# New durations and a table of priority shifts for a kernel's list scheduler

## The chip, the cores and the metric

The kernel runs on one core of one Trainium2 chip. The metric is the device time of one execution in microseconds (us). TensorE multiplies matrices into PSUM, VectorE and ScalarE work on tiles of 128 partitions, GpSimd does a few elementwise steps and issues small copies, SyncE (its queue is SP) issues most transfers. Each engine executes its own queue strictly in the order in which the program lists its instructions.

## The reference

Two transformer blocks in sequence on one sequence of 512 tokens with 1024 features, all in fp32. The first block has two layers. Layer one mixes with a chunked mLSTM of four heads, layer two with banded softmax attention of twelve heads; both also attend to 256 memory tokens with four heads of 64, and each ends in a convolutional gated feed-forward of width 2816. The second block has one layer: four differential attention heads (two softmaxes, the second taken away with a weight lambda), eight causal heads with a forget gate, and a gated feed-forward.

```python
for l in range(DEPTH):                       # first block, two layers
    h = rmsnorm(x, norm_mix_g[l])
    if l < N_A_LAYERS: ...                   # mLSTM heads, gated by sigmoid(o)
    else: mix_out = band_attention(q, k_pad, v_pad, b_rel_bias[bl])
    mem_out = memory_attention(q_mem, mem, mem_w_kv[l])
    x = x + jnp.concatenate([mix_out, mem_out], axis=-1) @ w_out
    x = x + conv_ffn(rmsnorm(x, norm_ffn_g[l]), ffn_w_up[l], ffn_conv_w[l], ffn_conv_b[l], ffn_w_down[l])
...
p = softmax(where(chunk_mask, s1, NEG)) - lam * softmax(where(chunk_mask, s2, NEG))   # second block
pf = softmax(where(causal, sf, NEG))
```

## The kernel before, in words

Activations stand with features on the partitions: a tile is 128 features by 512 tokens. A product of fp32 accuracy is made of three fp32r matmuls: each operand is split into a rounded upper half and the rest, and `mm3` (L423, L424, L425 in `mm3`; L443 to L445 in `tm`, for results with tokens on the partitions) multiplies upper by upper, upper by lower and lower by upper. Weights come in by SyncE's queue into two buffers (tag `wr`, L403), are rounded by ScalarE or VectorE (tag `wh`, `round`, L383) and have the rounded half taken away by VectorE or GpSimd (tag `wl`, `sub`, L371); both have four buffers.

`run` lays the program down stage by stage: memory keys and values, norm, first mixer (`layer_a`), output projection, feed-forward (`ffn`), the same with `layer_b`, then norms and `block2_attn`, output projection, feed-forward, last norm. In an attention head the scores (`scores`, L559 and L562) go through `softexp` (reduction L574, exponential L577, reciprocal L578), `scale` (L378), transposes (L589) and `put_pt` (L595 on ScalarE, L596 on VectorE), and `pv64` multiplies by the values (L608, L609, sum of two halves at L611 and L612). A key tile (`build_k`) is copied to the other partitions by two pairs of small transfers from GpSimd's queue (L551, L552).

What stands in each engine's queue is not the program order. The program is traced twice. In the first pass `Order` takes every instruction with its operands, gives each a duration (`duration`) and simulates the engines: an instruction becomes ready when its inputs are done plus a latency, and each engine that falls free takes the ready instruction with the lowest key among up to 60 whose tile buffers can be had (`can`: buffers of one tag are handed out in program order). The key is the position in the program plus what `prio` adds (50 for the first norm, 600 for one set of gates). Where an engine other than TensorE finds nothing, `other` lets it take a step that was made with `either` (round, sub, scale) from VectorE's or ScalarE's backlog. In the second pass the program is traced again with the engines so chosen, and the order of each engine is fixed.

Of the kernel before, what the change touches and what calls it, by code (L numbers as in the profile page):

```python
# [47 lines left out]
class Order:  # L48
# [7 lines left out]
    LAT = {"PE": 200, "DVE": 130, "Activation": 140, "Pool": 80, "SP": 0}  # L56
    SETS = {"Exp": "el", "Tanh": "e", "Silu": "s", "Sqrt": "q", "Ln": "l"}

    def __init__(self, nc, insts, bufs, flex, late):
# [3 lines left out]
        for ins in insts:  # L63
            e = ins.engine.name
            if e not in self.LAT or ins.opcode in ("TilePoolBoundary", "RegisterMove"):
                continue
            self.ops.append(ins)
# [7 lines left out]
        self.cost = [self.duration(k) for k in range(n)]  # L75
# [3 lines left out]
        self.key = [k + late.get(i.name, 0) for k, i in enumerate(self.ops)]  # L79
        self.deps()  # L80
        self.slots()

    @staticmethod
    def region(a):
        ap = a.bass_ap
        t = ap.tensor
        name = t.name
        if "dram" in str(ap.space).lower():
            tot = 1
            lo = hi = ap.offset  # L90
            for st, c in ap.ap:
                hi += st * (c - 1)
                tot *= c
            return (name, 0, 1, lo, hi + 1, tot, tot, a.dtype, False)
        ps = t.shape[1] if len(t.shape) > 1 else 1
        row = ap.ap[0][0] or 1
        p0, o = divmod(ap.offset, row)
        lo = hi = o
        free = 1
        for st, c in list(ap.ap)[1:]:  # L100
            hi += st * (c - 1)
            free *= c
        return (name, p0, p0 + ap.ap[0][1], lo, hi + 1, free, free * ap.ap[0][1], a.dtype, "PSUM" in str(ap.space).upper())

    def duration(self, k, e=None):
        ins, e = self.ops[k], e or self.eng[k]
        outs, rd = self.acc[k]
        n = outs[0][5]
        if self.dma[k]:
            return 475 if e == "SP" else 1016  # L110
        op = ins.opcode
        psum = any(r[8] for r in rd)
        scalars = sum(1 for r in rd if r[5] == 1) if n > 1 else 0
        if e == "PE":
            if rd[0][7] == F32R:
                return max(n * 0.4167 + 2.6, 107)
            return 109 if getattr(ins, "is_transpose", False) else max(4 * n * 0.4167, 214)
        if e == "DVE":
            if op == "Reciprocal":
                return 70 + 6.3 * n  # L120
            if op == "TensorReduce":
                return 67 + 1.04 * max(r[5] for r in rd)
            fast = op in ("TensorCopy", "Memset") or (op == "TensorScalarPtr" and len(rd) - scalars < 2)
# [3 lines left out]
        if op == "TensorTensor":  # L127
            return 150 + 2.1 * n
        if op == "Memset":
            return 35 + 0.83 * n  # L130
        return 165 + 0.83 * n + 80 * scalars
# [11 lines left out]
    def slots(self):  # L143

        import re
        self.tag, self.index, self.users = {}, {}, {}
        count = {}
        for k in range(len(self.ops)):
            names = {r[0] for rr in self.acc[k] for r in rr}
            for nm in names:  # L150
                m = re.match(r"([a-z]+)\d+_", nm)
                if not m or m.group(1) not in self.bufs:
                    continue
                if nm not in self.tag:
# [6 lines left out]
        self.mine = [[nm for nm in {r[0] for rr in self.acc[k] for r in rr} if nm in self.tag] for k in range(len(self.ops))]  # L161

    def run(self):
        n = len(self.ops)
        left = [len(p) for p in self.pred]
        ready = [0.0] * n
        engines = list(self.LAT)
        avail = {e: [] for e in engines}
        free_at = {e: 0.0 for e in engines}
# [4 lines left out]
        order = {e: [] for e in engines}  # L174
        ev = []
# [1197 lines left out]
```

## Time and profile before

| | us |
|---|---|
| median of 3 runs | 1928.72 (1928.42 to 1932.72) |
| the profiled execution | 1928.72 |
| its span, first to last instruction | 1926.9 |
| TensorE busy | 1850.2 |
| VectorE busy | 1187.1 |
| ScalarE busy | 868.3 |
| GpSimd busy | 323.3 |

Busy time of TensorE counts from the start of a matmul to its modelled end, and matmuls overlap; time in which any of them runs counts once. The granted clock is the share of full speed (2.4 GHz) that TensorE had; its lower level is 1.2 GHz.

### The profile page before, as it was taken

The page shows a single profiled execution, that of the slowest core. Times are in us where ns is not written, and L with a number is a line of the kernel's source. Part 1 is how long each engine was busy: PE and PEld are TensorE (multiplying, and loading weights), DVE is VectorE, ACT ScalarE, POOL GpSimd, SP SyncE. Part 2 cuts the span into 40 slices and gives each one's busy share as a digit, 9 for nine tenths or more (in the row PEclk, how much of TensorE's full clock was granted, in tenths as well). Part 3 has the DMA queues.
Part 4 walks back from the last instruction along what each step waited for, and adds up shares of the span by engine and source line. Part 5 has one row for each costly group of instructions (what it writes and reads, how often), then busy time and mean ns, then how long its engine had stood idle before and what let it go on. Part 6 is the DMA issues. An engine that isn't in the chain of part 4 may idle for free.

```text
span 1926.9 us, 23991 instructions
## 1 busy us (share of the span) xinstructions
PE 1850.2 (96%) x8628; PEld 1528.4 (79%) x8628; DVE 1187.1 (62%) x2233; ACT 868.3 (45%) x1651; POOL 323.3 (17%) x335
## 2 busy tenths in 40 slices
PE   7999899999999999889999999989998999999997
PEld 7887688888888878768888888878776788888885
DVE  6969776543555667696654455676989754434433
ACT  5567654432444555574443344344657533323332
POOL 2212111100111202131110011141443111001110
PEclk9999999999999999999999999999999999999998
DMA  5323232233323523323223322333321323232222
GB/s 184 93 93 105 83 98 91 95 94 103 99 92 112 160 92 114 88 79 126 98 99 91 103 92 90 98 120 111 94 80 42 110 98 98 89 101 95 98 89 86
DMA packets 59095, 191.93 MB, mean 100 GB/s; under 512 B 7776, under 2 KB 14304, under 8 KB 57184
## 3 DMA queue, kind: packets, MB, share of 16 engines
q1 hardware_dynamic: 54432, 177.81, 28.7%
q0 software_dynamic: 4544, 12.59, 2.6%
q8 instruction: 68, 1.11, 0.2%
q14 instruction: 51, 0.42, 0.1%
HBM read 174.64 MB, written 6.29 MB: 94 GB/s over the span
## 4 chain that ended last, share of the span: by engine, by line
PE 77%; DVE 9%; ACT 2%; issue 2%; DMA 1%; POOL 0%; DVEq 0%; ACTq 0%; SPq 0%; POOLq 0%
PE bd L423 23%; PE bd L424 23%; PE bd L425 23%; DVE ae L574 1%; DVE pt L596 1%; DVE ae L378 1%; PE bd L444 1%; PE bs L559 1%; PE bd L443 1%; PE bd L445 1%; PE bt L589 1%; DVE kq L371 1%; ACT ae L577 1%; DMA kq<-kq 1%; DVE wl L371 1%
## 5 line engine op out<-in xcount | busy, mean ns | idle before, releaser
L383 ACT CAST wh<-wr 128x512 fp32r<-128x512 f32 (+2 forms) x574 | 341.7, 596 | 787.2 <-PE bd L424 627.7
L423 PE MATMUL bd<-xs,wh 128*128 128x512 f32 (+1 forms) x1680 | 655.8, 391 | 9.2 <-ACT wh L383 8.2
L425 PE MATMUL bd<-xs,wl 128*128 128x512 f32 (+1 forms) x1680 | 655.2, 390 | 0.2 <-DVE wl L371 0.2
L424 PE MATMUL bd<-xs,wh 128*128 128x512 f32 (+1 forms) x1680 | 654.7, 390 | 0.0
L371 DVE TENSOR_TENSOR wl<-wr,wh 128x512 fp32r<-128x512 f32 (+2 forms) x590 | 398.0, 677 | 333.9 <-ACT wh L383 325.0
L423 PEld LDWEIGHTS bd<-xs,wh 128*128 128x128 f32 x1680 | 316.4, 188 | 74.5 <-ACT wh L383 8.2
L425 PEld LDWEIGHTS bd<-xs,wl 128*128 128x128 f32 x1680 | 316.7, 188 | 63.9 <-issue 1.2
L424 PEld LDWEIGHTS bd<-xs,wh 128*128 128x128 f32 x1680 | 316.7, 188 | 63.6 <-issue 1.9
L735 POOL TENSOR_TENSOR te<-te,R 128x512 f32<-128x512 f32 x66 | 85.8, 1300 | 825.3 <-ACT te L734 825.3
L423 PE MATMUL bd<-kq,wh 128*128 128x512 f32 x528 | 205.4, 389 | 0.0
L424 PE MATMUL bd<-pt,wh 128*128 128x512 f32 x528 | 205.4, 389 | 0.0
L425 PE MATMUL bd<-kq,wl 128*128 128x512 f32 x528 | 205.4, 389 | 0.0
L423 PEld LDWEIGHTS bd<-kq,wh 128*128 128x128 f32 x528 | 99.1, 188 | 20.6
L424 PEld LDWEIGHTS bd<-pt,wh 128*128 128x128 f32 x528 | 99.1, 188 | 20.6
L425 PEld LDWEIGHTS bd<-kq,wl 128*128 128x128 f32 x528 | 99.1, 188 | 20.6
L738 DVE TENSOR_TENSOR te<-bd,te 128x512 f32<-128x512 f32 x66 | 45.6, 691 | 104.5 <-PE bd L425 98.5
L723 DVE TENSOR_TENSOR te<-bd,R 128x512 f32<-128x512 f32 x66 | 45.6, 691 | 94.5 <-PE bd L425 94.5
L505 POOL TENSOR_TENSOR ae<-ae,ae 128x512 f32<-128x512 f32 x40 | 58.0, 1450 | 242.2 <-ACT ae L501 208.0
L371 POOL TENSOR_TENSOR wl<-wr,wh 128x512 fp32r<-128x512 f32 (+2 forms) x42 | 56.9, 1354 | 177.0 <-ACT wh L383 119.8
L383 ACT CAST kq<-te 128x512 fp32r<-128x512 f32 (+1 forms) x109 | 67.5, 620 | 38.3 <-DVE te L738 32.1
L589 PE MATMUL bt<-ident,ae 128*128 128x128 f32 x304 | 56.1, 285 | 22.9 <-DVE ae L378 9.7
L443 PE MATMUL bd<-wh,xs 128*128 128x384 f32 (+3 forms) x200 | 65.4, 333 | 6.4 <-ACT wh L383 3.4
(260 smaller groups left out, 2238.3 us busy)
## 6 DMA issues: line engine op xcount, KB each, us to landing
wr<-in_w_g SPq DMA_DIRECT2D x66, 512.0 KB, 3.3
wr<-in_w_u SPq DMA_DIRECT2D x66, 512.0 KB, 3.3
wr<-in_w_d SPq DMA_DIRECT2D x48, 512.0 KB, 3.4
wr<-in_w_d SPq DMA_DIRECT2D x48, 192.0 KB, 2.3
kq<-kq POOLq DMA_DIRECT2D x64, 128.0 KB, 3.2
wr<-in_w_qk SPq DMA_DIRECT2D x12, 512.0 KB, 3.2
v<-in_xT SPq DMA_DIRECT2D x4, 1024.0 KB, 8.6
wr<-in_w_o SPq DMA_DIRECT2D x8, 512.0 KB, 3.5
```

Source lines behind the costliest of these rows:

```text
L371: self.either("DVE", ("DVE", "Pool"), lambda e: e.tensor_tensor(out=out, in0=a, in1=b, op=ALU.subtract))
L378: return e.tensor_scalar(out=out, in0=a, scalar1=s, scalar2=1.0, op0=ALU.mult, op1=ALU.mult)
L383: self.either("Activation", ("DVE", "Activation"), lambda e: (e.copy if e is self.nc.scalar else e.tensor_copy)(out, a))
L423: mm(o, lhsT=wh, rhs=xh, start=start, stop=False)
L424: mm(o, lhsT=wh, rhs=xl, start=False, stop=False)
L425: mm(o, lhsT=wl, rhs=xh, start=False, stop=stop)
L443: mm(pss[b][:, :ncol], lhsT=x[k][0][:, tb], rhs=hi, start=st, stop=False)
L505: (nc.gpsimd if k < 6 else nc.vector).tensor_tensor(out=sq, in0=acc, in1=sq, op=ALU.add)
L589: self.nc.tensor.transpose(o[:, k * 128:(k + 1) * 128], p[:, k * 128:(k + 1) * 128], self.ident)
L723: nc.vector.tensor_tensor(out=g, in0=pg, in1=R, op=ALU.mult)
L735: nc.gpsimd.tensor_tensor(out=s, in0=s, in1=R, op=ALU.mult)
L738: nc.vector.tensor_tensor(out=h, in0=pu, in1=s, op=ALU.mult)
```

## The change

Only the planner and its inputs change; the instructions that compute are the same.

- `duration` returns three numbers: the time for which the engine is taken, the further time until the result is out, and whether the instruction uses the SBUF port that VectorE and GpSimd share. While one of the two is in an instruction of that kind, the other's does not start in the plan.
- The latency per producer (`LAT`) is replaced by one per consumer (`WAKE`); a result used on the same engine now waits too, except on TensorE and SyncE. A TensorE instruction that does not follow another at once is charged 85 ns more.
- The program is cut into numbered groups: methods marked `@group` and a few `with self.part()`. A group's number is its place in the order in which groups are entered, outer before inner; an instruction belongs to the innermost. `SHIFT` gives 142 of the groups two numbers, which are added to the keys of the group's TensorE instructions and of all its others.
- `diff_block` is a part of `block2_attn` made into a method, so that it can be a group.

```diff
-    LAT = {"PE": 200, "DVE": 130, "Activation": 140, "Pool": 80, "SP": 0}
+    WAKE = {"PE": 52, "DVE": 34, "Activation": 35, "Pool": 80, "SP": 27}
...
-            return 475 if e == "SP" else 1016
+            return (470, 0, 0) if e == "SP" else (530, 0, 0)
...
             if rd[0][7] == F32R:
-                return max(n * 0.4167 + 2.6, 107)
+                return max(n * 0.41667 + 13.3, 109), 164, 0
...
-            return 69 + (0.52 if fast and not psum else 1.04) * n + 61 * (scalars > 0)
+            if op == "ISA":
+                m = max([r[1] for r in rd] + [1])
+                return 69 + 1.04 * m + 107 if m > 1 else 20, 90, int(len(sb) > 1)
+            port = op != "Memset" and (len(sb) > 1 or (fast and len(sb) == len(big)))
+            return 69 + (0.52 if fast and not psum else 1.04) * n + 61 * (scal > 0), 88, int(port)
         if e == "Activation":
-            return (53 if psum else 93) + 0.8333 * n + 95 * scalars + 95 * (len(outs) > 1)
+            return (53 if psum else 93) + 0.8333 * n + 95 * scal + (95 if len(outs) > 1 else 0), 103, 0
...
+                if port:
+                    a, b = ("DVE", "Pool") if e == "DVE" else ("Pool", "DVE")
+                    s = max(s, lock[b])
+                    lock[a] = s + d
+                if e == "PE" and t > free_at[e] + 1:
+                    d += 85
...
-                    nb = self.acc[k][0][0][6] * 4
-                    s = max(t + c + 650, dma_free)
-                    dma_free = s + nb / 360.0
-                    end = dma_free + 1000
+                    b = max(s + d + (650.0 if e == "SP" else 900.0), dma_free)
+                    dma_free = b + self.acc[k][0][0][2] * 4 / 334.0
+                    end = dma_free + (900 if e == "SP" else 1100)
...
-                    elif self.eng[q] != e or self.dma[k]:
-                        r = end + lat + (60 if self.eng[q] == "PE" else 0)
+                    elif qe != e or self.dma[k]:
+                        r = end + self.WAKE[qe]
                     else:
-                        r = end + (60 if e == "DVE" else 0)
+                        r = s + d if e in ("PE", "SP") else end + self.WAKE[qe]
...
+    SHIFT = {
+        19: (-852, 0), 22: (-841, -866), 28: (215, 0), 39: (-131, 0), 42: (-30, 0), 45: (-121, 0), 50: (-96, 0),
...
+        231: (2470, 0), 235: (293, 0), 243: (-99, 0), 245: (711, 0), 255: (-1460, 0), 363: (2469, 0), 373: (2281, 0),
+        378: (0, -961), 398: (0, -1337), 419: (-164, 0), 420: (-124, 0), 423: (0, -403), 428: (0, -266),
...
+        1017: (285, 0),
+    }
...
+        a, b = self.SHIFT.get(me, (0, 0))
+        for i in self.nc.cur_bb.bb.instructions[n:]:
+            if i.name not in self.grp:
+                self.grp[i.name] = me
+                self.late[i.name] = self.late.get(i.name, 0) + (a if i.engine.name == "PE" else b)
```

## Rows read from the trace of the kernel before

**Rows 1.** The page's first part: busy time, share of span, instructions by engine.
```profile
span 1926.9 us, 23991 instructions
PE 1850.2 (96%) x8628; PEld 1528.4 (79%) x8628; DVE 1187.1 (62%) x2233; ACT 868.3 (45%) x1651; POOL 323.3 (17%) x335
```

**Rows 2.** Stretches: length; busy PE, PEld, DVE, ACT, POOL; clock; DMA share; GB/s.
```profile
8.00:50.00 42.00, 38.43 (x222) 35.45 (x223) 31.18 (x56) 24.35 (x48) 9.50 (x10) 1.00 0.45 163
50.00:243.00 193.00, 185.29 (x902) 151.47 (x901) 158.62 (x293) 119.28 (x241) 38.95 (x41) 0.98 0.29 92
243.00:690.00 447.00, 446.42 (x2039) 368.99 (x2038) 255.54 (x412) 191.35 (x337) 56.91 (x53) 1.00 0.33 103
690.00:862.00 172.00, 150.81 (x756) 126.16 (x755) 125.30 (x341) 97.60 (x235) 39.10 (x59) 0.95 0.33 95
862.00:1262.00 400.00, 400.00 (x1769) 330.63 (x1768) 225.62 (x333) 153.51 (x245) 45.92 (x34) 1.00 0.31 101
1262.00:1505.00 243.00, 220.42 (x1148) 179.19 (x1146) 202.75 (x518) 139.37 (x319) 88.07 (x96) 0.99 0.29 84
1505.00:1910.00 405.00, 405.00 (x1791) 334.81 (x1790) 178.10 (x271) 136.00 (x224) 43.99 (x33) 1.00 0.30 98
1910.00:1927.00 17.00, 3.80 (x14) 1.71 (x12) 7.64 (x12) 2.76 (x4) 0.00 (x0) 0.63 0.33 123
```

**Rows 3.** TensorE's waits, whole span: waiter <- releaser: us in total, times, longest.
```profile
PE bt L589 <- DVE ae L378: 9.7, 16, 1.3
PE bd L423 <- ACT wh L383: 8.2, 1, 8.2
```

**Rows 4.** Stretches of 10 us in the band attention, columns as in rows 2.
```profile
710.00:720.00 10.00, 6.45 (x29) 4.97 (x28) 6.21 (x11) 4.38 (x7) 0.00 (x0) 0.98 0.34 102
...
770.00:780.00 10.00, 8.53 (x54) 7.63 (x53) 9.84 (x30) 8.23 (x20) 4.26 (x8) 1.00 0.32 80
780.00:790.00 10.00, 6.67 (x41) 4.71 (x40) 8.95 (x31) 7.37 (x22) 2.24 (x4) 1.00 0.16 34
790.00:800.00 10.00, 7.76 (x28) 7.16 (x29) 3.85 (x7) 3.21 (x6) 0.61 (x1) 0.66 0.11 36
```

**Rows 5.** TensorE's waits from 1262 to 1505 us, the longest in total.
```profile
PE bt L493 <- DVE oa L489: 4.9, 2, 4.1
```

**Rows 6.** Stretches in the second block before and in its attention, columns as above.
```profile
1270.00:1300.00 30.00, 23.68 (x124) 21.46 (x123) 23.68 (x32) 12.30 (x22) 21.00 (x15) 0.94 0.40 133
1350.00:1360.00 10.00, 9.25 (x44) 7.27 (x44) 9.93 (x24) 5.81 (x12) 5.97 (x9) 1.00 0.23 52
```

**Rows 7.** The page: groups (busy us, mean ns | idle) and DMA issues (us to landing).
```profile
L423 PE MATMUL bd<-xs,wh 128*128 128x512 f32 (+1 forms) x1680 | 655.8, 391 | 9.2 <-ACT wh L383 8.2
...
wr<-in_w_g SPq DMA_DIRECT2D x66, 512.0 KB, 3.3
...
kq<-kq POOLq DMA_DIRECT2D x64, 128.0 KB, 3.2
```

**Rows 8.** Instructions of L371: ns shortest/median/longest, first and last start us.
```profile
L371 DVE TENSOR_TENSOR wl<-wr,wh x590: 432/684/1796, 8.4 to 1901.6; 128x512 fp32r<-128x512 f32 x151, 128x384 fp32r<-128x384 f32 x42, 128x392 fp32r<-128x392 f32 x2, 128x264 fp32r<-128x264 f32 x2
...
L371 POOL TENSOR_TENSOR wl<-wr,wh x42: 755/1298/1818, 59.9 to 1508.3; 128x512 fp32r<-128x512 f32 x32, 128x384 fp32r<-128x384 f32 x9, 128x264 fp32r<-128x264 f32 x1
```

**Rows 9.** Instructions of L383, ScalarE's casts of weights, columns as in rows 8.
```profile
L383 ACT CAST wh<-wr x574: 412/622/671, 7.5 to 1901.0; 128x512 fp32r<-128x512 f32 x151, 128x384 fp32r<-128x384 f32 x36, 128x264 fp32r<-128x264 f32 x3, 128x392 fp32r<-128x392 f32 x2
```

**Rows 10.** GpSimd's issues of copies within key tiles, columns as in rows 8.
```profile
L551 POOL DMA_DIRECT2D kq<-kq x40: 516/527/716, 70.4 to 1472.4; - x40
L552 POOL DMA_DIRECT2D kq<-kq x40: 518/518/569, 73.3 to 1474.5; - x40
```

**Rows 11.** ScalarE's waits from 690 to 862 us: total, times, longest.
```profile
ACT wh L383 <- PE bd L424: 14.7, 9, 2.6
```

**Rows 12.** The chain that ended last, around 745 us: start, us, what.
```profile
744.45 4.54 DMA kq<-kq
749.12 0.47 PE bs L559 x2
```

More of the change, by code (lines that the diff above doesn't have):

```diff
@@ L79, in __init__ @@
         self.key = [k + late.get(i.name, 0) for k, i in enumerate(self.ops)]
+        self.need = [self.SETS.get(str(getattr(i, "func", "")).split(".")[-1], "-") for i in self.ops]
+        self.cost = {}
+        for k in range(n):
+            for e in self.flex[k][1] if k in self.flex else (self.eng[k],):
+                self.cost[k, e] = self.duration(k, e)
         self.deps()
@@ L85, in region @@
         ap = a.bass_ap
[L86 to L99, printed above, removed]
+        free = rows = 1
@@ L118, in duration @@
+        sb = [r for r in big if not r[4]]
+        psum = any(r[4] for r in rd)
+        scal = len(rd) - len(big) if n > 1 else 0
+        if e == "PE":
+            if rd[0][3] == F32R:
+                return max(n * 0.41667 + 13.3, 109), 164, 0
+            if getattr(ins, "is_transpose", False):
+                return 109, 120, 0
+            return 2 * max(2 * n * 0.41667 + 1.5, 112), 164, 0
         if e == "DVE":
             if op == "Reciprocal":
-                return 70 + 6.3 * n
+                return 70 + 6.3 * n, 76, int(len(sb) > 1)
@@ L173, in run @@
         users = dict(self.users)
-        order = {e: [] for e in engines}
+        order = {e: [] for e in E}
         ev = []
@@ L226, in run @@
                 order[e].append(k)
-                self.start[k] = t
                 done += 1
+                s = t
+                d, more, port = self.cost[k, e]
+                if port:
[4 more added lines that the diff above has]
+                    d += 85
+                if e == "Activation" and table not in self.need[k] and self.need[k] != "-":
+                    table = self.need[k][0]
+                    d += 1295
+                self.start[k] = s
                 for nm in self.mine[k]:
@@ L266, in run, with group, g @@
                         seq += 1
-                        heapq.heappush(ev, (end + 60, seq, "free", self.tag[nm]))
-        assert done == n, (done, n, [(e, [(k, self.ops[k].opcode, [(nm, nm in held) for nm in self.mine[k]]) for _, k in avail[e][:4]]) for e in engines])
-        self.total = max(free_at.values())
-        return order
-    def other(self, e, t, avail, free_at, can):
-        for d in ("DVE", "Activation"):
-            wait = free_at[d] - t
-            if d == e or wait <= 0:
-                continue
-            for key, k in sorted(avail[d])[:40]:
-                if k in self.flex and e in self.flex[k][1] and wait + self.cost[k] > self.duration(k, e) + 100 and can(k):
-                    avail[d].remove((key, k))
-                    heapq.heapify(avail[d])
-                    self.choice[self.flex[k][0]] = e
-                    self.eng[k] = e
-                    self.cost[k] = self.duration(k)
-                    return k
-                wait += self.cost[k]
+                        heapq.heappush(ev, (end + 50, seq, "free", self.tag[nm]))
+        assert done == n, (done, n)
+        self.total = max(self.end)
+        return order
     def names(self):
         return [[self.ops[k].name for k in ks] for ks in self.run().values()]
+def group(f):
+    @functools.wraps(f)
+    def g(self, *a, **k):
+        with self.part():
+            return f(self, *a, **k)
+    return g
 class Build:
@@ L494, in bcast_col @@
         return o
+    @group
     def sumsq(self, xt):
@@ L744, in ffn @@
                 ps = self.fm(wd[half], m, hid)
-                nc.vector.tensor_tensor(out=x[m], in0=ps, in1=x[m], op=ALU.add)
+                with self.part():
+                    nc.vector.tensor_tensor(out=x[m], in0=ps, in1=x[m], op=ALU.add)
+    @group
     def v_evac_a(self, pss, col, gates=None):
@@ L780, in raw_gates @@
         return f
+    @group
     def gates_a(self):
```

185 lines of the change are left out of this document (111 added, 74 removed), and 18 rows, old and new, of the table SHIFT.

## The prediction

> **What bounds the kernel now.** I read the page first. TensorE works 1850.2 us of a span of 1926.9 us, VectorE 1187.1 us, ScalarE 868.3 us [rows 1]. So all that an order of instructions can change is the 76.7 us in which TensorE stands, plus the time in which it runs at the lower clock. The number of matmuls does not change, nor the operands of any instruction.
>
> The second view is the table of stretches [rows 2]; the reader is to see that the 76.7 us are not spread out. In the three feed-forward stretches (243 to 690, 862 to 1262, 1505 to 1910) TensorE idles 0.6, 0 and 0 us: 447, 400 and 405 us that no order makes shorter, because the matmuls follow one another without a gap there. Idle time, span minus busy: 8.0 us before 8 us and 3.6 from 8 to 50; 7.7 from 50 to 243 (first mixer); 21.2 from 690 to 862 (band attention); 22.6 from 1262 to 1505 (second block's attention); 13.2 after 1910 (final norm and output). In the three attention stretches the granted clock is 0.98, 0.95 and 0.99 of full speed, so up to 0.02 x 193 = 3.9, 0.05 x 172 = 8.6 and 0.01 x 243 = 2.4 us went to spells at 1.2 instead of 2.4 GHz; they come after idle time.
>
> What can an order not mend? The start (first matmul waits 8.2 us for the first cast weight [rows 3]), the tail (one dependent chain), and the chain of two norms after the second feed-forward: in 1270 to 1300 TensorE idles 30 - 23.7 = 6.3 us [rows 6], and the longest wait there is 4.1 us for the scaled identity of a norm [rows 5]. What is left in reach: 3.6 (start) + 7.7 + 3.9 (first mixer) + 21.2 + 8.6 (band attention) + 22.6 + 2.4 - 6.3 (second block) = 63.7 us. TensorE's rows overlap (390 ns long [rows 7], one every 400 / 1769 = 0.226 us in a full stretch [rows 2]), so a short wait can hide in a "busy" row; some us more may be in reach, and I leave them to the range.
>
> Why does TensorE stand there? The ten-us rows show two kinds [rows 4, 6]. In 770 to 790 and 1350 to 1360 VectorE is busy 9 to 9.9 of 10 us while TensorE idles 0.7 to 3.3 us: the projections that could have filled TensorE have already run, and the softmax waits for VectorE. In 710 to 720 and 790 to 800 VectorE itself has 4 to 6 us free: TensorE waits for a transfer, a PSUM bank or one dependent chain. VectorE as a whole is not the limit: busy 158.6 of 193, 125.3 of 172 and 202.8 of 243 us [rows 2], so 34, 47 and 40 us of slack, each larger than the idle time of TensorE in the same stretch. The waits by name are short: 16 of TensorE's for the scaled probabilities (L378), the longest 1.3 us, are its largest item after the start [rows 3].
>
> **The change, part by part.** (1) The prices. Arithmetic on the device is untouched; only the plan is made from other numbers. For a 128x512 fp32r matmul the plan took 216 ns, now 226.6 and 164 more until its result is out; the trace has 391 ns a row and one every 226 ns [rows 2, 7], so the new pair is right and the old plan believed TensorE 4.5% faster than it is. A 128x512 cast of a weight on ScalarE: old 519 + 140 + 60 = 719 ns until a matmul may start, new 519 + 103 + 52 = 674; the trace has a median of 622 for 519 + 103 [rows 9]. The subtraction behind it on VectorE: old 601 + 190 = 791, new 601 + 88 + 52 = 741; the trace has a median of 684 ns for 601 + 88 [rows 8]. Two dependent VectorE instructions: old +60, new +122. The issue of a small copy on GpSimd's queue: old 1016, new 530; the trace has 527 [rows 10]. Along one softmax block the corrections nearly cancel: +9 for the matmul, +107 for the reduction with its accumulator, +62 for each VectorE pair, -50 for each of the two steps back to TensorE, a few ns else: about +80 ns on some 4 us. So I cost new prices alone at 0. Bounds: the 11 ns by which each matmul was taken too short are 11 x (902 + 756 + 1148) = 31 us of TensorE time over the three stretches [rows 2], by which the plan and the chip could drift apart in either direction; drift is not loss, since most lies under slack of VectorE, and I keep a quarter, 8 us, to each side.
>
> (2) The port lock: in the new plan VectorE instructions with two SBUF inputs, and its fast ones, wait for a GpSimd instruction in progress, and the other way round. The row of the weight subtraction shows what is meant: median 684 ns, longest 1796, 1.1 us more than the median and so less than the 1.3 us of the same subtraction on GpSimd [rows 8]. As the median is undisturbed, I cost it at 0; it changes the plan's estimate, not the chip.
> The page Perfetto Trace Analysis of the Trainium skill, section Optimizing Scalar/DVE Operations, speaks against what the scheduler does with it: it says that moving work from VectorE to GpSimd may not help, since the two share a port. By that rule, if the new plan sends some 20 more scalings of 0.6 us to GpSimd, VectorE gets back none of the 12 us that the plan counts as free, and of a gain of 30 us that rests on 87 us of slack in the last two attention stretches 12 / 87 x 30 = 4 us would be missing (an estimate). The row's median says that most of such work runs undisturbed, so I subtract nothing.
>
> (3) The table. Its 142 keys number the groups in the order in which they are entered; counting the calls from the first stage on gives 1152 groups, and the keys fall on 39 groups of the first mixer, 6 of the first feed-forward, 44 of the band attention, 53 of the second block: 49 are softmax steps, 24 the writing of transposed probabilities, 10 scores, 24 projections of one tile. That is where the idle time lies. Of the entries for engines other than TensorE 66 pull forward and 24 push back: softmax work goes ahead of the weight casts and subtractions that share VectorE and ScalarE. Of the entries for TensorE, the sixth query projection of the band attention is pushed back by 2281 places: it is a filler of 8 x 3 matmuls, about 5.4 us, ahead of the idle time in 710 to 720 [rows 4]. A key only orders what is ready, and tiles of one name are still taken in program order, so a projection cannot overtake another; the order of scores, transposes and projections among each other can change.
> What it brings: at most the 63.7 us, at least less than nothing (rival two). Between the ends I go by the two kinds of idle time. The first kind (VectorE full, TensorE starved) goes where softmax work is spread into the stretches in which VectorE has slack; the second only where a filler is ready. I take half in each stretch: 1.8 of 3.6 at the start, 5.8 of 11.6 in the first mixer, 14.9 of 29.8 in the band attention, 9.3 of 18.7 in the second block, together 31.8; less 2 for the 6 keys in the feed-forward and for weight loads whose issue on SP's queue moves with the group (a transfer lands 3.3 us after its issue [rows 7], and two buffers of raw weights are all there is): 30 us.
> What is late next: VectorE. If the band attention loses 15 of 172 us, VectorE's share there goes from 73% to 80%; in the second block 9 of 243 take it from 83% to 87%. Neither is full.
>
> **The sum.** The profiled execution took 1928.72 us, which is also the median (span 1926.9 and 1.8 around it). 1928.7 - 30 = 1899 us.
>
> **Rivals.** One, no change: what is won in the plan does not come out on the chip because the idle time only changes place, for instance from waits for L378 to waits for weight subtractions (L371) that the pulled-forward softmax now stands ahead of. For it: ScalarE's casts already wait 14.7 us in the band attention for the matmul that frees a weight buffer, so casts and matmuls run there in lockstep [rows 11]; against it: 47 us of slack on VectorE. 1923 to 1934.
> Two, slower: the queues are strictly in order, and an engine that meets an instruction whose input is late holds all behind it. The place is the copy of half a key tile on GpSimd's queue (L551, L552), which the scores wait for. The chain of waits has 4.5 us from its first issue to the landing [rows 12]; new prices say 0.53 + 0.90 + 0.39 + 1.10 = 2.9 us from issue to landing, where the trace has a median of 3.2 [rows 7]. In that chain the first issue was at 744.45, the first score needs the second, which the plan has 0.53 us later, and the score began at 749.12 [rows 12]: 744.45 + 0.53 + 2.92 + 0.05 = 747.95 in the plan, 1.2 us earlier. If softmax steps and scores pulled forward leave no slack there, each of 20 key tiles (40 + 40 copies, four to a tile [rows 10]) costs TensorE 1.2 us, or 24 us, against some 10 us that are still won: 1928.7 + 14 = 1943. It decides where the first score of a head is placed less than 1.2 us behind the planned landing with no projection ahead of it.
> Three, much faster: nearly all of the reach comes in, as fillers and softmax mix evenly: 1928.7 - 60 = 1869. For it: every stretch has more slack on VectorE than TensorE has idle time; against it: scores, transposes and outputs share five PSUM banks and the weights four buffers, so work cannot run far ahead.
> That the table does nothing (numbers that miss their groups) is part of rival one; the count above speaks against it.
>
> **How the numbers follow.** Forecast (8 to 50 us won, 1879 to 1921): 0.62. Much faster: 0.13. No change: 0.12. Slower: 0.13. Predicted 1899. About 0.3% (5.8 us) is what a measurement of this kernel can tell from no change; so faster 0.75, same 0.12, slower 0.13. For the range I take in the third rival's 1869 and the bound of 8 us on the prices at the other end as far as 1934; some 0.05 is left out below and 0.12 above.
>
> **What would show it.** In the profile after: TensorE's busy time within 15 us of 1850 (less where spells at 1.2 GHz go), and the three feed-forward stretches 447, 400 and 405 us long as before; if those change, the gain is not where I put it. The band attention should shrink most, to about 157 us with a granted clock of 0.97 or more; the second block to about 234. VectorE's share in both goes up. If TensorE's waits name the key copies, rival two was right; if VectorE is at 9.5 or more through both stretches and TensorE still waits, the slack that I counted was not usable. I am wrong if idle time after 690 is still above 40 us.

## The result and the profile after

The changed kernel took 1895.2 us (median of 4 runs, 1893.6 to 1898.2) where the kernel before, measured beside it, took 1929.2: a ratio of 0.983 (95% interval 0.981 to 0.984), 1.7% faster. Forecast were 1899 us and a range of 1869 to 1934. The sum came out within 4 us. The experiments below show that two of its terms, near enough as totals, were wrong stage by stage in opposite directions, and that a term put at 0, the port lock, is one without which the gain is gone.

The page of the changed kernel, span and busy times by engine, answers to [rows 1]:

```profile
span 1891.8 us, 24049 instructions
PE 1837.0 (97%) x8628; PEld 1524.8 (81%) x8628; DVE 1158.2 (61%) x2168; ACT 876.7 (46%) x1678; POOL 355.9 (19%) x373
```

The profiled execution took 1893.6 us. The span is 35.1 us shorter. TensorE's idle time went from 76.7 to 1891.8 - 1837.0 = 54.8 us, 21.9 less; the other 13.2 us came out of TensorE's busy time with the same 8628 matmuls. VectorE has 28.9 us less to do, GpSimd 32.6 us more: the plan moved work, which the prediction names only as a possibility (some 20 more scalings) and counts at nothing.

The stretches of the changed kernel, cut where the stretches of [rows 2] now end (columns as there):

```profile
8.00:50.00 42.00, 40.76 (x235) 38.41 (x236) 29.96 (x58) 27.61 (x54) 10.67 (x11) 1.00 0.48 172
50.00:234.00 184.00, 178.53 (x890) 148.01 (x889) 151.52 (x286) 118.84 (x240) 35.84 (x41) 1.00 0.30 95
234.00:682.00 448.00, 447.62 (x2038) 368.53 (x2037) 258.67 (x406) 185.72 (x324) 66.26 (x62) 1.00 0.32 103
682.00:840.00 158.00, 144.01 (x757) 121.47 (x756) 117.30 (x321) 100.86 (x250) 49.84 (x72) 0.99 0.37 104
840.00:1240.00 400.00, 400.00 (x1769) 330.69 (x1768) 221.45 (x327) 156.99 (x250) 48.94 (x36) 1.00 0.32 101
1240.00:1470.00 230.00, 217.35 (x1148) 181.11 (x1147) 190.86 (x494) 143.96 (x331) 96.60 (x108) 0.99 0.30 88
1470.00:1875.00 405.00, 405.00 (x1790) 334.56 (x1788) 178.39 (x267) 135.98 (x224) 46.93 (x35) 1.00 0.31 98
1875.00:1892.00 17.00, 3.68 (x11) 1.98 (x10) 7.64 (x12) 2.76 (x4) 0.00 (x0) 0.58 0.33 123
```

Read it from the lengths: the three feed-forward stretches are 448, 400 and 405 us, where they were 447, 400 and 405. Of TensorE's idle time, 21.2 us in the band attention became 14.0, 22.6 us in the second block's attention 12.7, 7.7 us in the first mixer 5.5, 3.6 us at the start 1.2. The granted clock tells where the busy time went: 0.98, 0.95, 0.99 became 1.00, 0.99, 0.99, so by the working of the prediction 14.9 us lost to 1.2 GHz became about 0.01 x 158 + 0.01 x 230 = 3.9 (rough, as the shares have two digits). The idle time in front of those spells went, and the spells with it. VectorE's share is 74% and 83% in the last two attention stretches, as before (73% and 83%), not 80% and 87% as forecast: the stretch got shorter and VectorE's work with it.

For comparing kernels I use marks that do not depend on where a stretch is cut: the last add of an output projection and the last add of a feed-forward on VectorE. These rows give them for the kernel before (L699 and L745) and the changed one (L770 and L818): ns shortest/median/longest, then start of the first and of the last of eight adds.

```profile
L699 DVE TENSOR_TENSOR v<-bd,v x8: 679/684/692, 254.7 to 283.4; 128x512 f32<-128x512 f32 x8
L745 DVE TENSOR_TENSOR v<-bd,v x8: 691/692/692, 591.9 to 644.2; 128x512 f32<-128x512 f32 x8
L699 DVE TENSOR_TENSOR v<-bd,v x8: 678/682/692, 878.0 to 906.6; 128x512 f32<-128x512 f32 x8
L745 DVE TENSOR_TENSOR v<-bd,v x8: 691/692/692, 1215.3 to 1267.7; 128x512 f32<-128x512 f32 x8
L699 DVE TENSOR_TENSOR v<-bd,v x8: 679/682/692, 1521.1 to 1549.7; 128x512 f32<-128x512 f32 x8
```

```profile
L770 DVE TENSOR_TENSOR v<-bd,v x8: 680/684/692, 245.5 to 274.2; 128x512 f32<-128x512 f32 x8
L818 DVE TENSOR_TENSOR v<-bd,v x8: 691/692/692, 584.2 to 636.5; 128x512 f32<-128x512 f32 x8
L770 DVE TENSOR_TENSOR v<-bd,v x8: 682/686/692, 855.5 to 884.1; 128x512 f32<-128x512 f32 x8
L818 DVE TENSOR_TENSOR v<-bd,v x8: 691/692/692, 1192.8 to 1245.1; 128x512 f32<-128x512 f32 x8
L770 DVE TENSOR_TENSOR v<-bd,v x8: 682/685/692, 1485.5 to 1514.1; 128x512 f32<-128x512 f32 x8
```

The differences of the last starts are the lengths of the stages (new prices alone is the first experiment below). Each column is one execution; for new prices alone it is the fastest of ten, 2.4 us below their median:

| stage, us | before | new prices alone | changed | forecast gain | gain | of it by the table |
|---|---|---|---|---|---|---|
| start and first mixer | 283.4 | 276.7 | 274.2 | 7.6 | 9.2 | 2.5 |
| first feed-forward | 360.8 | 361.1 | 362.3 | 0 | -1.5 | -1.2 |
| band attention | 262.4 | 256.2 | 247.6 | 14.9 | 14.8 | 8.6 |
| second feed-forward | 361.1 | 361.1 | 361.0 | 0 | 0.1 | 0.1 |
| second block's attention | 282.0 | 289.9 | 269.0 | 9.3 | 13.0 | 20.9 |
| last feed-forward to the end | 377.2 | 377.2 | 377.7 | 0 | -0.5 | -0.5 |

The waits of TensorE by name answer to [rows 3] (waiter <- releaser: us in total, times, longest):

```profile
PE bd L475 <- ACT wh L435: 8.3, 1, 8.3
PE bo L675 <- ACT pt L661: 4.6, 8, 1.5
PE bt L654 <- DVE ae L430: 3.5, 8, 0.8
...
PE bo L497 <- DVE xs L679: 1.4, 1, 1.4
...
PE bs L623 <- DMA kq<-kq: 0.7, 1, 0.7
```

The wait for the first weight is as long as it was. The wait of the transposes for the scaled probabilities went from 9.7 us in 16 waits to 3.5 in 8. The key copies, the place of the rival that ended slower, hold TensorE once, for 0.7 us.

Where the remaining idle time lies is seen in stretches of 10 us of the changed kernel, first of the band attention, then of the second block's attention (columns as in [rows 4]):

```profile
740.00:750.00 10.00, 10.00 (x58) 8.45 (x57) 9.42 (x36) 9.84 (x30) 7.28 (x10) 1.00 0.46 125
...
760.00:770.00 10.00, 9.89 (x65) 8.66 (x64) 9.61 (x36) 9.11 (x28) 5.76 (x10) 1.00 0.20 54
770.00:780.00 10.00, 6.44 (x30) 4.87 (x31) 6.12 (x14) 4.71 (x12) 1.20 (x2) 0.93 0.10 28
...
820.00:830.00 10.00, 7.43 (x45) 5.45 (x43) 9.24 (x31) 9.60 (x29) 5.83 (x7) 1.00 0.40 102
```

```profile
1340.00:1350.00 10.00, 10.00 (x48) 8.04 (x48) 9.20 (x39) 8.97 (x23) 4.59 (x8) 1.00 0.24 53
...
1430.00:1440.00 10.00, 8.47 (x55) 6.72 (x53) 9.53 (x32) 9.80 (x28) 8.46 (x11) 1.00 0.21 48
```

In the rows from 740, 760 and 1340 VectorE is as full as it was in [rows 4] (9.2 to 9.6 of 10), but TensorE now is full too: projections are left to run beside the softmax. At the end of each stage (820 to 840, 1420 to 1470) almost none is left, and TensorE has 1.1 to 2.6 us of idle time in each 10: 4.5 of the 14.0 us in the band attention, 6.7 of the 12.7 in the second block. The largest gap of the band attention lies elsewhere: 3.6 us from 770 to 780, where VectorE has 4 us free and TensorE waits for single steps, the longest 1.4 us for the output of a head (xs, L679).

### The profile page after: what moved, and what is told of

Its sections match the earlier page's. It is cut to its first block, busy times and chain, and to the rows that moved or that the text cites. A ratio compares the mean times of both kernels' runs of the same rounds, so it can differ in the third digit from the quotient of the medians.

```text
span 1891.8 us, 24049 instructions
## 1 busy us (share of the span) xinstructions
PE 1837.0 (97%) x8628; PEld 1524.8 (81%) x8628; DVE 1158.2 (61%) x2168; ACT 876.7 (46%) x1678; POOL 355.9 (19%) x373
## 4 chain that ended last, share of the span: by engine, by line
PE 79%; DVE 4%; ACT 3%; issue 2%; DMA 1%; POOL 0%; SPq 0%; DVEq 0%; ACTq 0%; POOLq 0%
PE bd L475 24%; PE bd L476 24%; PE bd L477 24%; ACT ae L642 1%; PE bt L654 1%; PE bd L497 1%; PE bd L499 1%; PE bd L498 1%; ACT pt L661 1%; DVE ae L639 1%; PE bt L539 1%; PE bs L623 1%; ACT kq L435 1%; DVE pt L662 1%; DMA wr<-in_w_ao 0%
## 5 line engine op out<-in xcount | busy, mean ns | idle before, releaser
L435 ACT CAST wh<-wr 128x512 fp32r<-128x512 f32 (+2 forms) x583 | 347.0, 596 | 782.5 <-PE bd L476 644.8
L423 DVE TENSOR_TENSOR wl<-wr,wh 128x512 fp32r<-128x512 f32 (+3 forms) x586 | 403.2, 690 | 343.3 <-ACT wh L435 333.3
L423 POOL TENSOR_TENSOR wl<-wr,wh 128x512 fp32r<-128x512 f32 (+3 forms) x46 | 60.6, 1318 | 237.2 <-ACT wh L435 92.7
L498 PE MATMUL bd<-wl,xs 128*128 128x384 f32 (+3 forms) x200 | 65.3, 327 | 0.9 <-DVE wl L423 0.9
```

The source lines that it names most:

```text
L423: self.either("DVE", ("DVE", "Pool"), lambda e: e.tensor_tensor(out=out, in0=a, in1=b, op=ALU.subtract))
L435: self.either("Activation", ("DVE", "Activation"), lambda e: (e.copy if e is self.nc.scalar else e.tensor_copy)(out, a))
L498: mm(pss[b][:, :ncol], lhsT=x[k][0][:, tb], rhs=l, start=False, stop=False)
```

## The experiments

All are kernels with the same arithmetic; only the order of the queues, and the engine of some round, sub and scale steps, differ. Ratios are to the kernel before, with 95% intervals.

The theory of the prediction, A: the table carries the gain by a better order; prices alone and the port lock are worth 0. Rivals: B, the prices carry it; C, any loosening of the program order does; D, the table's entries work only one after the other; E, the gain is work taken off VectorE. A has two readings: A1, the table states urgencies that hold under any prices; A2, it is fitted to one plan.

**New prices alone**

```diff
-    SHIFT = {
-        19: (-852, 0), 22: (-841, -866), 28: (215, 0), 39: (-131, 0), 42: (-30, 0), 45: (-121, 0), 50: (-96, 0),
...
-    }
+    SHIFT = {}
```

> The new prices and the port lock, with an empty table (SHIFT = {}). Theory A (the table carries the gain, the prices alone are worth 0 within 8 us either way): 1921 to 1937 us, and the three mixing stages about as long as before. Rival B (the prices carry it: a plan that knows the durations leaves less idle time by itself): 1893 to 1905 us, and the table adds under 8 us. A value between 1905 and 1921 shares the gain between the two.

Measured: 1926.4 us, ratio 0.999 (0.998 to 0.9999). A holds and B falls as far as the sum goes. But the sum is made of parts that are not 0 (the same marks):

```profile
L747 DVE TENSOR_TENSOR v<-bd,v x8: 679/684/692, 248.1 to 276.7; 128x512 f32<-128x512 f32 x8
L795 DVE TENSOR_TENSOR v<-bd,v x8: 690/692/692, 585.4 to 637.8; 128x512 f32<-128x512 f32 x8
L747 DVE TENSOR_TENSOR v<-bd,v x8: 680/683/692, 865.4 to 894.0; 128x512 f32<-128x512 f32 x8
L795 DVE TENSOR_TENSOR v<-bd,v x8: 691/692/692, 1202.7 to 1255.1; 128x512 f32<-128x512 f32 x8
L747 DVE TENSOR_TENSOR v<-bd,v x8: 680/683/692, 1516.4 to 1545.0; 128x512 f32<-128x512 f32 x8
```

Against before, the first mixer is 6.7 us shorter, the band attention 6.2 shorter, the second block's attention 7.9 longer (last starts, as in the table above). Two things became worse there. The first is seen on the page and in a VectorE group of the second block, the difference of two softmaxes that follows a GpSimd scaling; the groups' columns are busy us, mean ns, and idle time with its releaser, first this kernel's two lines, then the same group before and in the changed kernel.

```profile
PE 1844.7 (96%) x8628; PEld 1532.1 (80%) x8628; DVE 1178.4 (61%) x2168; ACT 873.0 (45%) x1669; POOL 375.4 (20%) x382
...
L1077 DVE SCALAR_TENSOR_TENSOR ae<-ae,sm,ae 128x128 f32<-128x128 f32 (+3 forms) x16 | 16.0, 1010 | 2.3 <-POOL ae L1075 2.3
```

```profile
L1080 DVE SCALAR_TENSOR_TENSOR ae<-ae,sm,ae 128x128 f32<-128x128 f32 (+3 forms) x16 | 12.1, 758 | 0.6 <-POOL ae L1078 0.6
```

```profile
L1100 DVE SCALAR_TENSOR_TENSOR ae<-ae,sm,ae 128x128 f32<-128x128 f32 (+3 forms) x16 | 12.4, 790 | 1.7 <-POOL ae L1098 1.6
```

With new prices GpSimd works 375.4 us, 52.1 more than before, and VectorE only 8.7 less: 65 instructions left its queue, but some that stayed took longer, in this group 1010 ns in the mean where before it was 758. With the table GpSimd works 32.6 us more than before and VectorE 28.9 less, and the same group takes 790. Most of the longer time is one step. These two rows of new prices alone give the group's shortest, median and longest step in ns, and two GpSimd subtractions (start, us for both) within the longest, which began at 1345.67:

```profile
L1077 DVE SCALAR_TENSOR_TENSOR ae<-ae,sm,ae x16: 336/742/3259, 1334.7 to 1433.7; 128x128 f32<-128x128 f32 x4, 128x256 f32<-128x256 f32 x4, 128x384 f32<-128x384 f32 x4, 128x512 f32<-128x512 f32 x4
...
1345.86 2.50 POOL L400 TENSOR_TENSOR wl<-wr,wh 128x512 fp32r<-128x512 f32 x2
```

All 16 steps together cost VectorE 3.9 us more than before. That they cost the kernel as much is not shown, and another thing weighs more: the chain on VectorE that makes the forget gates' operands (`cb`), for which the scores wait. The three fences have the stretch of that chain with new prices alone (and the ten us behind it), before, and in the changed kernel (columns as in [rows 4]), each with TensorE's wait for its end.

```profile
1442.00:1449.00 7.00, 2.21 (x3) 0.66 (x3) 6.78 (x12) 0.00 (x0) 0.00 (x0) 0.50 0.00 0
1450.00:1460.00 10.00, 7.77 (x33) 6.70 (x33) 7.26 (x26) 7.22 (x19) 3.99 (x6) 0.72 0.12 27
...
PE bs L602 <- DVE cb L1200: 4.0, 1, 4.0
```

```profile
1446.00:1454.00 8.00, 6.74 (x29) 4.93 (x28) 7.75 (x13) 2.58 (x4) 1.22 (x1) 1.00 0.27 84
...
PE bs L561 <- DVE cb L1138: 1.3, 1, 1.3
```

```profile
1416.00:1424.00 8.00, 7.52 (x33) 5.51 (x31) 7.50 (x16) 2.19 (x4) 1.00 (x1) 1.00 0.19 49
...
PE bs L625 <- DVE cb L1223: 0.5, 1, 0.5
```

With new prices alone no projection is left to run beside the chain: TensorE idles 4.8 of 7 us, where it was 1.3 of 8 before and 0.5 of 8 in the changed kernel, and the granted clock is 0.50 there and 0.72 in the ten us behind. Together that is some 6 of the 7.9 us (an estimate: 4.8 - 1.3 = 3.5 of idle time and 0.28 x 10 = 2.8 of clock). GpSimd does nothing in those 7 us, so the shared port has no part in that wait.

**The table under the old prices**

```diff
 class Order:
...
-    WAKE = {"PE": 52, "DVE": 34, "Activation": 35, "Pool": 80, "SP": 27}
+    LAT = {"PE": 200, "DVE": 130, "Activation": 140, "Pool": 80, "SP": 0}
...
-                return max(n * 0.41667 + 13.3, 109), 164, 0
+                return max(n * 0.4167 + 2.6, 107)
...
```

> The planner of before (old durations, no port lock, old latencies) with the whole table. Theory A1 (the table says what work is urgent, and this holds under any prices): most of the gain, 1895 to 1910 us. Theory A2 (each entry was fitted to one plan, and means something else when the ready times move by tens of ns): 1918 to 1945 us. Under rival B, where prices carry the gain, about 1929 us.

Measured: 1927.7 us, ratio 0.999 (0.998 to 1.000). The table alone does nothing measurable either: A1 falls, and the time is what A2 forecast. Prices and table are each worth 0.1%, together 1.7%.

**Each entry given to the next group**

```diff
-    SHIFT = {
-        19: (-852, 0), 22: (-841, -866), 28: (215, 0), 39: (-131, 0), 42: (-30, 0), 45: (-121, 0), 50: (-96, 0),
...
+    SHIFT = {20: (-852, 0), 23: (-841, -866), 29: (215, 0), 40: (-131, 0), 43: (-30, 0), 46: (-121, 0), 51: (-96, 0),
...
```

> New prices, and every entry of the table given to the next group (number + 1): same numbers, same count, same stages, but a shift meant for a softmax step falls on the scores or the transposes next to it. Theory A (the entries fit their groups): the gain is gone, 1918 to 1950 us. Rival C (any such loosening of the program order does it, the values hardly matter): 1893 to 1908 us.

Measured: 1930.1 us, ratio 1.001 (1.000 to 1.002). The same numbers one group further give nothing: the entries fit their groups, and C falls for this displacement, the only other assignment of the whole table that was run.

**Only the second block's entries**

```diff
-    SHIFT = {
-        19: (-852, 0), 22: (-841, -866), 28: (215, 0), 39: (-131, 0), 42: (-30, 0), 45: (-121, 0), 50: (-96, 0),
...
-        583: (21, 0), 584: (0, 1737), 733: (0, -369), 738: (0, -194), 773: (0, -984), 779: (0, -80), 793: (0, -904),
...
+    SHIFT = {733: (0, -369), 738: (0, -194), 773: (0, -984), 779: (0, -80), 793: (0, -904),
...
```

> New prices with only the 53 entries of the second block's attention; the entries of the first mixer, the first feed-forward and the band attention are left out. Theory A (the stages are separate, as the feed-forwards between them leave nothing over): the first two stages as with new prices alone, the third as in the changed kernel, so 269 instead of 290 us from the last add of the second feed-forward to the last add of the output projection: 1926.4 - 21 = 1905 us (1901 to 1910). Rival D (an entry is right only in the state that the earlier ones leave): above 1915 us.

Measured: 1906.6 us, ratio 0.989 (0.987 to 0.990), where adding by stages gave 1905. The stage itself takes 1525.2 - 1255.4 = 269.8 us here, as in the changed kernel (269.0):

```profile
L795 DVE TENSOR_TENSOR v<-bd,v x8: 691/692/692, 1203.0 to 1255.4; 128x512 f32<-128x512 f32 x8
...
L747 DVE TENSOR_TENSOR v<-bd,v x8: 681/684/692, 1496.6 to 1525.2; 128x512 f32<-128x512 f32 x8
```

D falls for stages: what one gains is not given back or made larger by another. The 53 entries of the second block give two thirds of what the table gives.

**One price moved by 3 ns**

```diff
-    WAKE = {"PE": 52, "DVE": 34, "Activation": 35, "Pool": 80, "SP": 27}
+    WAKE = {"PE": 52, "DVE": 37, "Activation": 35, "Pool": 80, "SP": 27}
```

> The changed kernel with one price moved by 3 ns: VectorE's wake-up 37 instead of 34 ns, in the plan only. Theory A2 (the table is fitted to one plan, step by step): a good part of the gain goes, 1905 to 1930 us. Theory A1 (the table states urgencies that hold for any plan near this one): 1892 to 1900 us.

Measured: 1894.0 us, ratio 0.982 (0.981 to 0.984): all of the gain stays, and what A2 forecast here did not come. But 3 ns hardly change the plan: in the trace 8565 of TensorE's 8628 matmuls stand in the same place of its queue, by line and tiles, and no engine has an instruction more or less on the page. So the run shows that the gain is not an accident of one exact queue, and says little about plans that differ more.

**Work moved and order, apart**

The first kernel chooses the engines in a plan with the table, then empties the table and plans the order anew with these engines:

```diff
...
+    choice = trace(bacc, arrays, None, dbg)[0][1]
+    table, Build.SHIFT = Build.SHIFT, {}
+    plan = trace(bacc, arrays, None, dbg, choice)[0]
...
```

> Round, sub and scale steps sit on the engines that the plan with the table chose (VectorE 29 us less than before, GpSimd 33 us more); the order is planned anew with these engines and without the table. Theory A (the gain is the order): 1918 to 1932 us. Rival E (the gain is the work taken off VectorE): 1893 to 1908 us.

Measured: 1921.3 us, ratio 0.996 (0.994 to 0.997). The other way round, the engines are chosen with an empty table and the order is planned with the full one:

```diff
...
+    table, Build.SHIFT = Build.SHIFT, {}
+    choice = trace(bacc, arrays, None, dbg)[0][1]
+    Build.SHIFT = table
+    plan = trace(bacc, arrays, None, dbg, choice)[0]
...
```

> The reverse: round, sub and scale steps on the engines that the plan without the table chose, the order planned with these engines and with the table, no step moved any more. Theory A (the gain is the order, whatever engine does these steps): 1893 to 1908 us. Rival E, or the fitted plan A2 (moved steps and order belong together): 1915 to 1935 us.

Measured: 1921.0 us, ratio 0.996 (0.994 to 0.997). Each half is worth 0.3% beyond prices alone, the whole table 1.6%, so neither A nor E is borne out. But the two runs do not separate engines from order cleanly. Both plan a second time with every engine fixed, so that no step is taken from another engine's backlog any more, and no run plans in this way with both the engines and the table of the changed kernel. That the second planning itself loses the gain is a rival that no run excludes.

**The table's two halves**

One kernel keeps the first number of each entry (for TensorE) and has 0 for the second:

```diff
-    SHIFT = {
-        19: (-852, 0), 22: (-841, -866), 28: (215, 0), 39: (-131, 0), 42: (-30, 0), 45: (-121, 0), 50: (-96, 0),
...
+    SHIFT = {19: (-852, 0), 22: (-841, 0), 28: (215, 0), 39: (-131, 0), 42: (-30, 0), 45: (-121, 0), 50: (-96, 0),
...
```

> New prices with the TensorE half of the table (56 entries: when a projection, a score or a transpose goes); all other engines keep the program's own keys. Theory F (an order of fillers on TensorE is what closes the idle time): 1895 to 1908 us. Theory G (softmax work ahead of weight casts on VectorE and ScalarE closes it): 1918 to 1930 us. If the two halves belong together: both halves give less than half of the 31 us that the table is worth, so 1912 to 1927 here.

The other has 0 for the first number and keeps the second:

```diff
-    SHIFT = {
-        19: (-852, 0), 22: (-841, -866), 28: (215, 0), 39: (-131, 0), 42: (-30, 0), 45: (-121, 0), 50: (-96, 0),
...
+    SHIFT = {22: (0, -866), 69: (0, -454), 98: (0, -747), 102: (0, -13), 104: (0, -169),
...
```

> New prices with the other half (90 entries for VectorE, ScalarE, GpSimd and the transfers). Theory G: 1895 to 1908 us. Theory F: 1918 to 1930 us. If the halves belong together: 1912 to 1927 us, and the gains of the two halves do not add up to 31 us.

Measured: TensorE's half 1924.7 us, ratio 0.998 (0.997 to 0.999); the other half 1914.2 us, ratio 0.994 (0.992 to 0.996). Beyond prices alone that is 0.1% and 0.5%, against 1.6% for the whole. The halves belong together. When softmax work goes on VectorE, ScalarE and GpSimd matters more than when a projection goes on TensorE, but this alone is a third of the table's worth.

**Single prices taken back, with the whole table**

First the port lock, then the price of a matmul.

```diff
-                if port:
+                if False:
```

> The changed kernel, whole table, with a plan that lets VectorE and GpSimd use the shared port at the same time. Was cost at 0 in the prediction. If the lock is only a correction of a few ns on average, like the 3 ns of wake-up: 1892 to 1900 us. If the plan needs it (because the moved steps on GpSimd and VectorE's casts collide on the chip, or because the table was fitted to it): 1908 to 1930 us.

Measured: 1928.2 us, ratio 1.000 (0.998 to 1.001): the whole gain is gone.

```diff
-                return max(n * 0.41667 + 13.3, 109), 164, 0
+                return max(n * 0.41667 + 2.6, 109), 164, 0
```

> The changed kernel, whole table, with the old matmul price (10.7 ns less for each, 4.5% of a 128x512 matmul); all other prices new. If the matmul price is what the table leans on, since it sets how much vector work fits beside a projection: 1910 to 1930 us. If not: 1892 to 1902 us.

Measured: 1913.1 us, ratio 0.992 (0.991 to 0.994): somewhat more than half of it is gone.

Does the lock matter on the chip, because collisions at the port take the time? The page and the groups of the kernel without the lock say no. Of two groups that read two SBUF tiles, one got shorter (694 ns in the mean against 790 in the changed kernel, 16 times: 1.5 us less) and one longer (the sums of squares, 821 against 688, 16 times: 2.1 us more); neither is near 33 us. VectorE is busy 17.5 us more, with 39 instructions more, and GpSimd 15.8 us less: fewer steps were moved. That is 0.45 us for each further instruction, less than the 0.53 us (1158.2 / 2168) of VectorE's mean instruction, so its steps did not get longer on the whole. First the page's line and the two groups without the lock, then the second of them in the changed kernel.

```profile
PE 1855.4 (96%) x8628; PEld 1530.8 (79%) x8628; DVE 1175.7 (61%) x2207; ACT 863.1 (45%) x1650; POOL 340.1 (18%) x362
...
L1100 DVE SCALAR_TENSOR_TENSOR ae<-ae,sm,ae 128x128 f32<-128x128 f32 (+3 forms) x16 | 11.1, 694 | 2.0 <-POOL ae L1098 1.8
...
L564 DVE TENSOR_TENSOR ae<-ae,ae 128x512 f32<-128x512 f32 x16 | 13.1, 821 | 3.7 <-ACT ae L560 2.4 <-POOL ae L564 1.2
```

```profile
L564 DVE TENSOR_TENSOR ae<-ae,ae 128x512 f32<-128x512 f32 x16 | 11.0, 688 | 2.7 <-ACT ae L560 2.7
```

**Neither lock nor table**

```diff
-    SHIFT = {
-        19: (-852, 0), 22: (-841, -866), 28: (215, 0), 39: (-131, 0), 42: (-30, 0), 45: (-121, 0), 50: (-96, 0),
...
-    }
+    SHIFT = {}
...
-                if port:
+                if False:
```

> New prices without the port lock and with an empty table: the fourth corner beside the changed kernel (lock and table, 1895 us), new prices alone (lock, no table, 1926 us) and the table without the lock (1928 us). If leaving out the lock costs time by itself, because the chip's port collisions then hit steps that the plan counts on: 1940 to 1960 us, some 30 us more than with the lock, as the table showed. If the lock is worth nothing by itself and the table only fits the plan that it was made for: 1920 to 1932 us.

Measured: 1931.8 us, ratio 1.0015 (1.0006 to 1.0025). The four corners:

| us | without the table | with the table |
|---|---|---|
| without the lock | 1931.8 | 1928.2 |
| with the lock | 1926.4 | 1895.2 |

The lock is worth 5 us without the table and 33 with it; the table 4 us without the lock and 31 with it. So the lock is not by itself what saves the time: the table is a set of corrections to the plan with the lock.

**What the plan itself forecasts**

The planner's simulation has an end of its own (`self.total` in `Order.run`). It is no time of the chip. Worked out from these kernels, it tells what the table is worth in each plan, beside what it was worth on the chip:

| us | plan without the table | plan with it | worth in the plan | worth on the chip |
|---|---|---|---|---|
| new prices and lock | 1897.6 | 1864.0 | 33.6 | 31.2 |
| new prices, no lock | 1866.5 | 1858.5 | 8.0 | 3.6 |
| old prices | 1773.6 | 1769.1 | 4.5 | 1.5 |

So in the other two plans the table is worth little before the chip comes in. Its parts, under new prices and lock, are worth in the plan (and on the chip): given to the next group 2.3 us (3.7 lost), TensorE's half 9.5 (1.7), the other half 12.3 (12.2), the second block's entries 15.4 (19.8). None comes near the whole in either. And leaving out the lock makes the plan 31 us shorter without the table (1897.6 to 1866.5) where the chip's time rose by 5, so the plan without the lock counts on time that the chip does not give.

The same end bears on the rival in "Work moved and order, apart". Planned a second time with the engines fixed, the plan ends at 1882.1 us even with the engines and the whole table of the changed kernel, 18 us later than the changed kernel's own; the two kernels that were run end at 1889.5 and 1893.4. So a good part of what they lost may be the second planning. The control itself was not run on the chip.

## Why the prediction came out

**What bounds the kernel** was right. Idle time of TensorE in the three attention stretches, and the spells at the lower clock that follow it, were the whole of the reach; the feed-forward stages gave nothing and lost at most 1.5 us. Of the 63.7 us in reach 35 came in, 55%. The half that I took was a choice that no row gave, and that it came so near is luck. The sign of being wrong, more than 40 us of idle time after 690, stayed away only just: in the changed kernel it is 14.0 + 12.7 + 13.1 = 39.8 us after 682.

**One exclusion was wrong in part.** I took 6.3 us of idle time in 1270 to 1300, with its chain of norms, out of the reach. In the changed kernel that work lies some 22 us earlier, and the 50 us around it have 3.2 us of idle time:

```profile
1250.00:1300.00 50.00, 46.80 (x280) 44.11 (x279) 31.89 (x56) 22.36 (x49) 19.96 (x15) 0.97 0.39 129
```

At least half of that idle time could be filled, 3.1 us, and the second block gained 3.7 us more than forecast (13.0 instead of 9.3).

**Term 1, prices alone at 0 within 8 us,** measured 0.1% or 3 us, but by cancelling: 6.7 and 6.2 us won in two stages, 7.9 lost in a third. The argument that the corrections cancel along a softmax chain was not what happened. What I had left out is that prices also decide which steps go to GpSimd (52 us more of its time), and what is left for the end of a stage: in the second block the chain of the forget gates stood with no projection beside it, and TensorE idled 4.8 of 7 us. Here the rule of the page Perfetto Trace Analysis of the Trainium skill (section Optimizing Scalar/DVE Operations), that moving work from VectorE to GpSimd may not help since they share a port, agrees with the trace: 52.1 us more on GpSimd, 8.7 us less on VectorE. In the changed kernel the trade is 32.6 for 28.9, so the rule is a warning there and no bar. I subtracted nothing for it; no run shows what it cost in time.

**Term 2, the port lock at 0,** is the step that failed. "It changes the plan's estimate, not the chip" holds in that VectorE's steps did not get longer without the lock, and it does not follow that it is worth 0: the table's entries improve the plan made with that estimate (33.6 us in it) and hardly the one without (8.0). On the chip the lock is worth 33 us beside the table, and without it nothing of the gain is left. The sum stayed right because the changed kernel has both.

**Term 3, the table:** right that it falls on the groups where the idle time lies and that the numbers fit their groups. By stage it was mis-sized: I gave it 7.6, 14.9 and 9.3 us, it has 2.5, 8.6 and 20.9; the prices have the difference. And "the operands of no instruction change" hid that the engines of the flexible steps do; how much of the gain is theirs is not settled, since the two runs on it also plan in another way. I had counted on VectorE getting fuller as the stretches shrank. It stayed at 74% and 83%, since its work shrank as well.

**The rivals.** "No change" is what 6 of 12 variants near this change did: prices alone and the table alone each lie within 0.2% of before. No row that I had read from before told that the two need each other. "Slower" through the key copies: the chain still has two of them where it had three. The longer one, in the band attention, took 4.3 us, and TensorE ran projections beside it and waited 0.7 us for it:

```profile
733.37 4.31 DMA kq<-kq
```

"Much faster" fell in good part to the ends of the stages, where almost no projection is left to run beside VectorE, and in the band attention to gaps like the one from 770 to 780.

**Open.** Whether a table fitted to a plan without the lock would reach the same time was not tried, so how far the lock's truth about the chip matters, beyond 5 us, is not settled. Nor is it shown how far the moved steps and how far the order make the gain, nor why about half of it goes with 10.7 ns less for each matmul. That 3 ns more of wake-up cost nothing fits a plan that stayed nearly the same.

## What to carry to other kernels

A list of priorities and the prices of the planner that it was found with belong together: apart, each was worth next to nothing here. A changed price that changed the plan (the lock, 10.7 ns for each matmul) took all or half of the gain, and 3 ns that left the plan nearly the same took none. So when a price is corrected, ask the planner's own forecast whether the priorities still help, and find them again if not. Before predicting what a better order brings, take idle time and lower clock by stage, leave out the stages in which TensorE runs without a gap, and ask how much of the rest has independent matmuls ready beside it; here about half came in, and much of what stayed lies at the ends of the stages, where almost none are left. And ask of a new price not only whether it orders differently, but whether it moves work to another engine.

## What the runs showed of the hardware that was not expected

Where GpSimd had more of the elementwise steps, a few of VectorE's own got much longer: 16 steps that read two SBUF tiles took 758 ns in the mean before, 1010 with 52 us more of GpSimd work, 790 with 33 us more in another order. The longest took 3259 ns, where the median of its group is 742, and two GpSimd subtractions ran one after the other within it. And closing gaps of a few us on TensorE paid more than half as much again: 21.9 us less idle time came with 13.2 us less busy time for the same 8628 matmuls. About 11 us of that is the granted clock by the two-digit shares of the stretches (14.9 us lost to its lower level before, 3.9 after), and about 9 us by the shares of the whole spans, 0.990 and 0.994, less the last 17 us.
